# First transfers, first casts and query transposes regrouped in a two-layer decoder trunk

## The chip, the cores and the metric

The kernel runs on one core of a Trainium2 chip. The metric is device time in microseconds (us) of one execution; lower is better. Three runs of the kernel before gave 434.49, 434.71 and 436.08 us, median 434.71 us. Engines are named as the profile names them: PE is the matrix engine (PEld its weight loads), DVE the vector engine, ACT the scalar engine, POOL the GpSimd engine, and SPq the queue of SyncE, which issues most transfers. L12 is line 12 of the kernel before, unless said otherwise.

## What is computed

Two pre-norm mixer layers on x (256 tokens by 1024, float32), then a final RMSNorm. Cut to what matters here:

```python
h = rms_norm(x, norm_g)                       # layer 0
(nq, nkc, nvc, nks, nvs, nkw, nvw, ng, nz, mq, mk, mv, mz, eq, ez) = split(h @ w_in)
a_out = nsa_attention(rot(nq), kc, vc, rot(nks), nvs, rot(nkw), nvw, gates)   # 8 heads, 3 branches
b_out = moba_attention(rot(mq), rot(mk), mv)                                 # 8 heads
m_out = memory_attention(eq, mem_n, w_mem_kv)
x = x + concat(a_out * silu(nz), b_out * silu(mz), m_out * silu(ez)) @ w_out
# layer 1: retention (4 heads) and memory attention, the same outer form; then rms_norm
```

All inputs and the output are float32, and all projections go through PE with each float32 operand split in two.

## The kernel before, in words

**Arithmetic.** A float32 operand is split into a high part (`hi`, a cast to fp32r) and a low part (`lo`, the remainder, again fp32r). A product of two split operands is three matmuls, hi by hi, hi by lo and lo by hi (`mm3`, L243 to L247). For weights, `split` (L141) and, later, `fetch` and `finish` (L157, L170) have ACT write `whi` and then DVE write `wlo`. For x, `gain_cast` (L341) has ACT write `xh`, which is x transposed times the norm's gain, and `gain_low` (L345) has DVE write `xl`. Both are kept in tiles called `big`. The 1024 rows of the contraction are 8 k-tiles of 128.

**The head.** vec (gains, biases), x (transposed) and the weights of the first projection (`ksw`, keys and values of two branches, one half megabyte per two k-tiles) come in by the transfers of L380 to L394: vec and the first two k-tiles of x from ACT's queue, all else from SPq. Six matmuls on a zeroed tile (L397) run on PE meanwhile. Then the loop at L404 to L414 does, for each pair q of k-tiles: two `gain_cast`, two `gain_low`, then for each of the two k-tiles `split` and two `mm3` (token tiles 0 and 1, into the PSUM banks s0 and s1). After each pair but the first, ACT squares the pair before (`square`, L399); POOL adds the squares up (L493, L494), from which the reciprocal root mean square comes by way of PE and DVE, and then computes the angles of layer 1's rotary tables (L485 to L465, helper `angles`). The first pair's casts and the small angle work of layer 0 (L475 to L465 on DVE) share DVE with this loop.

**Buffers.** `raw` (6 buffers) holds transferred pieces, `whi` and `wlo` 4 buffers each. A transfer into a buffer waits on SPq until the buffer's last reader is done. Transfers also take eight completion semaphores in turn: the ninth transfer waits for the landing of the first, and so on.

**Slots.** From L978 on, PE's program is a row of projections. A projection is a generator that yields once per slot (half of a weight unit, 12 matmuls); at each yield `turn` (L188) advances the side tasks, which add their ACT, DVE and PE work at that place. Every engine's order is the order in which the program is written (`manual_schedule`), and each engine works its own list in order. `heads` (L546) is the side task that rotates and transposes queries and keys: per token tile three DVE instructions (`rotate`, L327), then `pause(HP)`, HP = 2 slots, then four PE transposes (L324), then, a slot later, an ACT copy (L556). `sparse_queries` (L722) starts one for the first attention's queries, whose transposes fall into the projection `sparse_gates` that follows; `block_queries` and `block_keys` start two more. `block_values` (L932) leaves its product in two `pj` banks (there are three), and its side task has ACT move both to SBUF (L939); the next projection, `block_gates`, needs one of these banks for its second half.

Of the kernel before, what the change touches and what calls it, by code (L numbers as in the profile page):

```python
# [13 lines left out]
AF = mybir.ActivationFunctionType  # L14
ALU = mybir.AluOpType
AX = mybir.AxisListType

P = 128
T = 256
D = 1024  # L20
KT = 8
# [3 lines left out]
MANUAL = {mybir.EngineType.DVE, mybir.EngineType.Activation, mybir.EngineType.PE, mybir.EngineType.Pool, mybir.EngineType.SP}  # L25
AHEAD = 2
DEPTH = 4
HP = 2
NRAW = 6
NS = 8  # L30
CUT = 256
# [22 lines left out]
V_G0 = 0  # L54
# [8 lines left out]
def trunk(  # L63
# [19 lines left out]
    nc = tc.nc  # L83
    sb = ctx.enter_context(tc.tile_pool(name="sb", bufs=1))
    pp = ctx.enter_context(tc.tile_pool(name="pp", bufs=4, space=bass.MemoryType.PSUM))
    V, S, G, PE = nc.vector, nc.scalar, nc.gpsimd, nc.tensor
# [17 lines left out]
    def load(t, src):  # L104
        nc.sync.dma_start(t, src)
        return t
# [34 lines left out]
    def split(raw, cols):  # L141

        hi = tl("whi", [P, 1024], NB, F32R)[:, :cols]
        lo = tl("wlo", [P, 1024], NB, F32R)[:, :cols]
        S.copy(hi, raw)
        V.tensor_tensor(lo, raw, hi.bitcast(F32), ALU.subtract)
        return hi, lo
# [38 lines left out]
    waiting, first, active, made, slot, free = deque(), [], [], set(), [0], {}  # L186
# [41 lines left out]
    def pause(n):  # L228

        for _ in range(n):  # L230
            yield
# [6 lines left out]
    def making(task, *names):  # L238

        yield from task  # L240
        made.update(names)

    def mm3(ps, lh, ll, rh, rl, start, stop, shared=False):  # L243

        PE.matmul(ps, lh, rh, start=start, stop=False, skip_group_check=shared)  # L245
        PE.matmul(ps, lh, rl, start=False, stop=False, skip_group_check=shared)  # L246
        return PE.matmul(ps, ll, rh, start=False, stop=stop, skip_group_check=shared)  # L247
# [93 lines left out]
    def gain_cast(raw, g, hi, k0, kts):  # L341
        for kt in kts:
            S.activation(hi[:, kt], raw[:, kt - k0], AF.Copy, scale=g[:, kt : kt + 1])  # L343

    def gain_low(raw, g, hi, lo, k0, kts):  # L345
        for kt in kts:
            V.scalar_tensor_tensor(lo[:, kt], raw[:, kt - k0], g[:, kt : kt + 1], hi[:, kt].bitcast(F32),  # L347
                                   op0=ALU.mult, op1=ALU.subtract)
# [4 lines left out]
    vect = tl("vec", [P, V_END])  # L353
# [8 lines left out]
    xh = tl("big", [P, KT, T], 4, F32R)  # L362
# [16 lines left out]
    posr = tl("yf", [P, T], 2, I32)  # L379
    with tc.manual_schedule(engines={mybir.EngineType.SP, mybir.EngineType.Activation}):  # L380
        nc.scalar.dma_start(vect, vec)
        load(wraw[0][:, 0:512], w512[2][:, 0:512])
        for k in range(2):
            nc.scalar.dma_start(xraw[0][:, k : k + 1], xT[:, k : k + 1])
        load(wraw[0][:, 512:1024], w512[2][:, 512:1024])
        S.activation(seed, seed, AF.Sin)
        for q in range(1, 4):
            load(xraw[q // 2][:, 2 * (q % 2) : 2 * (q % 2) + 2], xT[:, 2 * q : 2 * q + 2])
            load(wraw[q], w512[2 + q // 2][:, (q % 2) * 1024 : (q % 2 + 1) * 1024])
        load(cpak, cst)  # L390
        load(posi, pos)
        load(posr, posrow.to_broadcast([P, T]))
        for u in range(4):
            raws.append(load(tl("raw", [P, 1024], NRAW)[:, :560], w280[u // 2][:, u % 2 * 560 : u % 2 * 560 + 560]))  # L394
# [6 lines left out]
        S.activation(squares[q // 2][:, q % 2], xraw[q // 2][:, 2 * (q % 2) : 2 * (q % 2) + 2].rearrange("p k t -> p (k t)"), AF.Square)  # L401

    with tc.manual_schedule(engines=MANUAL):
        for q in range(4):  # L404
            gain_cast(xraw[q // 2], vect[:, V_G0 : V_G0 + 8], xh, 4 * (q // 2), range(2 * q, 2 * q + 2))
            gain_low(xraw[q // 2], vect[:, V_G0 : V_G0 + 8], xh, xl, 4 * (q // 2), range(2 * q, 2 * q + 2))
            for j in range(2):
                wh, wl = split(wraw[q][:, j * 512 : (j + 1) * 512], 512)
                kt = 2 * q + j
                for tok in range(2):  # L410
                    ts = slice(tok * P, (tok + 1) * P)
                    mm3(ps_k[tok], xh[:, kt, ts], xl[:, kt, ts], wh, wl, kt == 0, kt == KT - 1)
            if q:
                square(q - 1)  # L414

    rstd0 = tl("rstd0", [P, 2])
# [126 lines left out]
    szn = tl("v4", [P, 4, T], NV)  # L543


    def heads(ps, name, dst):  # L546

        for tok in range(2):
            while "tab" + name not in made:
                yield  # L550
            r = rotate(ps[tok], tabs[name][0][:, tok], tabs[name][1][:, tok], 8, 32)
            yield from pause(HP)
            tag, = yield from take()
            b = transposes([r[:, i * P : (i + 1) * P] for i in range(4)], tag)
            yield
            S.copy(dst[:, :, tok * P : (tok + 1) * P], b.rearrange("p (k t) -> p k t", t=P))  # L556
            give(tag)
# [164 lines left out]
    def sparse_queries():  # L722
        nonlocal qT
        ps = yield from project((xh, xl))
        qT = tl("v4", [P, 4, T], NV)
        active.append(making(heads(ps, "q", qT), "qT"))

    def compress():
        nonlocal gates, kcBD, vcR
# [202 lines left out]
    def block_values():  # L932
        nonlocal mvt
        ps = yield from project((xh, xl))
        mvt = tl("v4", [P, 2, 512], NV)

        def post():
            for tok in range(2):
                S.activation(mvt[:, tok], ps[tok], AF.Copy, scale=rstd0[:, tok : tok + 1])  # L939
            yield  # L940

        active.append(making(post(), "mvt"))
# [379 lines left out]
```

## Time and profile before

| | |
|---|---|
| median of three runs | 434.71 us (434.49, 434.71, 436.08) |
| profiled execution, its own time | 436.0 us |
| span of its instructions | 434.2 us, granted PE clock 0.992 |
| PE busy | 420.6 us, 97% of the span |
| first matmul of the first projection | starts at 9.38 us |
| first matmul of the second projection that waits (L246, pj) | starts at 23.53 us |
| query transposes of the first attention | start at 46.59 and 54.37 us |

The profile is of one execution. The timeline lists start and duration of instructions, per engine, and in brackets how long the engine stood idle before it and which work ended the idle time. The list of waits adds these up. The chain of waits goes back from the last instruction to whatever released each one.

### The profile page before, as it was taken

What the parts mean: (1) busy time and instruction counts of PE and PEld (TensorE: products, weight loads), DVE (VectorE), ACT (ScalarE), POOL (GpSimd) and SP (SyncE); (2) the same over time, 40 slices, a digit from 0 to 9 for tenths busy, and PEclk for the clock granted to TensorE, in tenths of its full rate; (3) what the DMA queues carried; (4) which work ended last, traced back from release to release, by engine and by line L of the source; (5) the groups of instructions that cost most, each with busy time, mean ns of one, the idle gap of its engine ahead of it and who ended that gap; (6) DMA issues with size and microseconds to landing.
All of it is one profiled execution on the core that took longest, in us unless ns stands there. A gap on an engine that the chain in (4) does not pass through costs nothing.

```text
span 434.2 us, 7030 instructions
## 1 busy us (share of the span) xinstructions
PE 420.6 (97%) x2622; PEld 363.0 (84%) x2622; DVE 307.7 (71%) x666; ACT 243.1 (56%) x453; POOL 18.0 (4%) x24
## 2 busy tenths in 40 slices
PE   6989999999999999999999999999999999999994
PEld 4878888788798987879999988888998888888883
DVE  2897979789597683759777675586887467685634
ACT  4748357676877574737437434646344444545703
POOL 0492000000000000000000000000000000000000
PEclk9899999999999999999999999999999999999998
DMA  8595643444667444526553536555454555655202
GB/s 269 175 329 183 251 163 107 141 141 148 196 206 274 151 109 162 161 85 198 162 195 114 172 131 188 193 201 164 146 171 167 182 190 189 203 171 178 80 0 97
DMA packets 22081, 73.18 MB, mean 169 GB/s; under 512 B 2720, under 2 KB 4000, under 8 KB 22048
## 3 DMA queue, kind: packets, MB, share of 16 engines
q1 hardware_dynamic: 21328, 72.04, 50.2%
q10 hardware_dynamic: 720, 0.71, 0.6%
q8 instruction: 20, 0.33, 0.3%
q14 instruction: 13, 0.11, 0.1%
HBM read 71.69 MB, written 1.05 MB: 168 GB/s over the span
## 4 chain that ended last, share of the span: by engine, by line
PE 84%; DVE 6%; POOL 3%; ACT 2%; DMA 2%; issue 1%; ACTq 0%; DVEq 0%; POOLq 0%
PE pj L245 22%; PE pj L247 21%; PE pj L246 21%; PE o L117 3%; PE s L117 2%; DVE wlo L174 2%; PE t L324 2%; PE s L324 2%; DMA raw<-in_xT 2%; PE s L246 1%; PE s L247 1%; PE tr L245 1%; PE tr L246 1%; PE tr L247 1%; PE s L245 1%
## 5 line engine op out<-in xcount | busy, mean ns | idle before, releaser
L174 DVE TENSOR_TENSOR wlo<-raw,whi 128x1024 fp32r<-128x1024 f32 (+1 forms) x118 | 142.5, 1211 | 63.0 <-ACT whi L166 60.9
L166 ACT CAST whi<-raw 128x1024 fp32r<-128x1024 f32 (+1 forms) x118 | 121.7, 1036 | 89.6 <-PE pj L247 38.3
L245 PE MATMUL pj<-whi,big 128*128 128x512 f32 (+2 forms) x256 | 97.4, 383 | 0.0
L246 PE MATMUL pj<-wlo,big 128*128 128x512 f32 (+2 forms) x256 | 96.1, 375 | 0.8 <-DVE wlo L174 0.8
L247 PE MATMUL pj<-whi,big 128*128 128x512 f32 (+2 forms) x256 | 95.9, 375 | 0.0
L245 PE MATMUL pj<-big,whi 128*128 128x256 f32 x256 | 73.6, 288 | 0.6 <-ACT v L939 0.6
L247 PE MATMUL pj<-big,wlo 128*128 128x256 f32 x256 | 72.6, 284 | 0.0
L246 PE MATMUL pj<-big,whi 128*128 128x256 f32 x256 | 72.5, 283 | 0.0
L245 PEld LDWEIGHTS pj<-whi,big 128*128 128x128 f32 x256 | 48.2, 188 | 9.3 <-issue 1.5
L246 PEld LDWEIGHTS pj<-wlo,big 128*128 128x128 f32 x256 | 48.3, 189 | 8.8 <-DVE wlo L174 1.1
L247 PEld LDWEIGHTS pj<-whi,big 128*128 128x128 f32 x256 | 48.2, 188 | 8.7
L245 PEld LDWEIGHTS pj<-big,whi 128*128 128x128 f32 x256 | 49.0, 191 | 2.7 <-issue 1.8
L246 PEld LDWEIGHTS pj<-big,whi 128*128 128x128 f32 x256 | 49.0, 191 | 0.1
L247 PEld LDWEIGHTS pj<-big,wlo 128*128 128x128 f32 x256 | 49.0, 191 | 0.0
L610 ACT ACTIVATE p<-p,mx 128x128 f32<-128x128 f32 (+1 forms) x48 | 21.2, 443 | 4.5 <-DVE mx L597 4.4
L245 PE MATMUL pj<-whi,y 128*128 128x512 f32 x42 | 16.9, 407 | 0.0
L247 PE MATMUL pj<-whi,y 128*128 128x512 f32 x42 | 16.4, 391 | 0.0
L246 PE MATMUL pj<-wlo,y 128*128 128x512 f32 x42 | 16.2, 391 | 0.0
L347 DVE SCALAR_TENSOR_TENSOR big<-raw,vec,big 128x256 fp32r<-128x256 f32 x16 | 7.8, 526 | 8.0 <-ACT big L343 8.0
L572 DVE TENSOR_SCALAR p<-p,sm 128x256 f32<-128x256 f32 (+1 forms) x48 | 12.7, 322 | 0.6
L570 ACT ACTIVATE p<-p,sm 128x256 f32<-128x256 f32 (+1 forms) x16 | 7.8, 489 | 7.9 <-DVE sm L566 7.5
L597 DVE CUSTOM_DVE_ANT_0 p<-s,cst 128x128 f32<-128x128 f32 (+1 forms) x24 | 7.1, 354 | 5.8 <-PE s L117 5.8
(350 smaller groups left out, 668.4 us busy)
## 6 DMA issues: line engine op xcount, KB each, us to landing
raw<-in_w SPq DMA_DIRECT2D x91, 512.0 KB, 3.9
raw<-in_wout SPq DMA_DIRECT2D x28, 512.0 KB, 4.2
raw<-in_w SPq DMA_DIRECT2D x4, 280.0 KB, 2.9
v<-in_w SPq DMA_DIRECT2D x2, 512.0 KB, 5.9
raw<-in_memT SPq DMA_DIRECT2D x2, 512.0 KB, 3.8
raw<-in_memtok SPq DMA_DIRECT2D x2, 512.0 KB, 4.8
v<-in_xtok SPq DMA_DIRECT2D x2, 512.0 KB, 5.5
v<-in_grow SPq DMA_DIRECT2D x2, 512.0 KB, 6.8
```

What stands on the lines that cost most here:

```text
L117: ins = PE.matmul(out, lhs, rhs, start=start, stop=stop)
L166: S.copy(hi, raw)
L174: V.tensor_tensor(lo, raw, hi.bitcast(F32), ALU.subtract)
L245: PE.matmul(ps, lh, rh, start=start, stop=False, skip_group_check=shared)
L246: PE.matmul(ps, lh, rl, start=False, stop=False, skip_group_check=shared)
L247: return PE.matmul(ps, ll, rh, start=False, stop=stop, skip_group_check=shared)
L324: PE.transpose(b[:, i * P : (i + 1) * P], a, ident)
L347: V.scalar_tensor_tensor(lo[:, kt], raw[:, kt - k0], g[:, kt : kt + 1], hi[:, kt].bitcast(F32), op0=ALU.mult, op1=ALU.subtract)
L570: S.activation(p[:, hh, a], p[:, hh, a], AF.Copy, scale=sm[:, hh, tok : tok + 1])
L572: V.tensor_scalar(p[:, hh, a], p[:, hh, a], sm[:, hh, tok : tok + 1], None, op0=ALU.mult)
L597: V.tensor_tensor_reduce(ps[i][:, hh, a], ss[i][hh][:, a], cpak[:, C_CAUSAL + a.start : C_CAUSAL + a.stop], -1.0, 3e38, ALU.add, ALU.min, ...
L610: S.activation(ps[i][:, hh, a], src, AF.Exp, bias=ms[i][:, hh, tok : tok + 1], scale=-1.0 if causal else 1.0, accum_out=ns[i][:, hh, tok : ...
```

## The change

Four edits, and one that only renames:

1. The first two k-tiles of x come in one transfer of 256 KB from ACT's queue instead of two of 128 KB; it is issued in the place of the first. SPq's list of transfers is as before, but since there is one transfer less, the semaphores that they wait for shift by one.
2. The loop of the head goes k-tile by k-tile: `split`, one `gain_cast`, one `gain_low`, and then the six matmuls with the token tile as the inner loop (hi by hi for both token tiles, then lo of the weights, then lo of x).
3. The queries of the first attention pause three slots instead of two before each pair of transposes; all others stay at two (the constant HP becomes a default argument).
4. In `block_values` DVE moves the first token tile's product, ACT the second.

```diff
-HP = 2
...
         nc.scalar.dma_start(vect, vec)
+        nc.scalar.dma_start(xraw[0][:, 0:2], xT[:, 0:2])
         load(wraw[0][:, 0:512], w512[2][:, 0:512])
-        for k in range(2):
-            nc.scalar.dma_start(xraw[0][:, k : k + 1], xT[:, k : k + 1])
         load(wraw[0][:, 512:1024], w512[2][:, 512:1024])
...
-        for q in range(4):
-            gain_cast(xraw[q // 2], vect[:, V_G0 : V_G0 + 8], xh, 4 * (q // 2), range(2 * q, 2 * q + 2))
-            gain_low(xraw[q // 2], vect[:, V_G0 : V_G0 + 8], xh, xl, 4 * (q // 2), range(2 * q, 2 * q + 2))
-            for j in range(2):
-                wh, wl = split(wraw[q][:, j * 512 : (j + 1) * 512], 512)
-                kt = 2 * q + j
+        for kt in range(KT):
+            q, j = kt // 2, kt % 2
+            wh, wl = split(wraw[q][:, j * 512 : (j + 1) * 512], 512)
+            gain_cast(xraw[q // 2], vect[:, V_G0 : V_G0 + 8], xh, 4 * (q // 2), (kt,))
+            gain_low(xraw[q // 2], vect[:, V_G0 : V_G0 + 8], xh, xl, 4 * (q // 2), (kt,))
+            for i, (x, w) in enumerate(((xh, wh), (xh, wl), (xl, wh))):
                 for tok in range(2):
-                    ts = slice(tok * P, (tok + 1) * P)
-                    mm3(ps_k[tok], xh[:, kt, ts], xl[:, kt, ts], wh, wl, kt == 0, kt == KT - 1)
-            if q:
+                    PE.matmul(ps_k[tok], x[:, kt, tok * P : (tok + 1) * P], w, start=kt == 0 and i == 0,
+                              stop=kt == KT - 1 and i == 2)
+            if q and j:
                 square(q - 1)
...
-    def heads(ps, name, dst):
+    def heads(ps, name, dst, wait=2):
...
-            yield from pause(HP)
+            yield from pause(wait)
...
-        active.append(making(heads(ps, "q", qT), "qT"))
+        active.append(making(heads(ps, "q", qT, 3), "qT"))
...
         def post():
-            for tok in range(2):
-                S.activation(mvt[:, tok], ps[tok], AF.Copy, scale=rstd0[:, tok : tok + 1])
+            V.tensor_scalar(mvt[:, 0], ps[0], rstd0[:, 0:1], None, op0=ALU.mult)
+            S.activation(mvt[:, 1], ps[1], AF.Copy, scale=rstd0[:, 1:2])
             yield
```

**ACT at the start of the program**, before. raw_76 is x's first half, raw_77 the weights of the first two k-tiles, raw_78 those of the next two, big_72 is `xh`:

```order
L381 DMA vec_63<-in_vec 128x104
L384 DMA raw_76<-in_xT 128x256 x2
L386 ACT_TABLE_LOAD
L386 ACTIVATE seed_61<-seed_61 128x1
L343 ACTIVATE big_72<-raw_76,vec_63 128x256 x2
L145 CAST whi_82<-raw_77 128x512
L145 CAST whi_144<-raw_77 128x512
```

And with the change (whose lines from L380 to L399 stand one or two lower):

```order
L380 DMA vec_63<-in_vec 128x104
L381 DMA raw_76<-in_xT 128x512
L384 ACT_TABLE_LOAD
L384 ACTIVATE seed_61<-seed_61 128x1
L144 CAST whi_82<-raw_77 128x512
L342 ACTIVATE big_72<-raw_76,vec_63 128x256
L144 CAST whi_141<-raw_77 128x512
L342 ACTIVATE big_72<-raw_76,vec_63 128x256
```

The first weight cast now stands ahead of x's first cast, and the second of each behind the first pair.

**DVE at the end of the head**, before. big_73 is `xl`, wlo_209 and wlo_219 belong to the last two k-tiles, wlo_243 to the first unit of the second projection; tmp and posf are layer 0's angles:

```order
L475 CAST posf_234<-pos_64 128x2
L347 SCALAR_TENSOR_TENSOR big_73<-raw_79,vec_63,big_72 128x256
L477 TENSOR_SCALAR tmp_27_90<-cst_65,posf_234 128x32 x2
L146 TENSOR_TENSOR wlo_209<-raw_81,whi_208 128x512
L456 TENSOR_SCALAR tmp_54_231<-tmp_27_90 128x64
L146 TENSOR_TENSOR wlo_219<-raw_81,whi_218 128x512
L457 TENSOR_SCALAR tmp_54_231<-tmp_54_231 128x64
L461 SCALAR_TENSOR_TENSOR tmp_27_90<-tmp_54_231,tmp_27_90 128x64
L174 TENSOR_TENSOR wlo_243<-raw_114,whi_242 128x560
```

With the change:

```order
L473 CAST posf_233<-pos_64 128x2
L145 TENSOR_TENSOR wlo_204<-raw_81,whi_203 128x512
L475 TENSOR_SCALAR tmp_27_90<-cst_65,posf_233 128x32 x2
L346 SCALAR_TENSOR_TENSOR big_73<-raw_79,vec_63,big_72 128x256
L145 TENSOR_TENSOR wlo_216<-raw_81,whi_215 128x512
L454 TENSOR_SCALAR tmp_54_230<-tmp_27_90 128x64
L346 SCALAR_TENSOR_TENSOR big_73<-raw_79,vec_63,big_72 128x256
L455 TENSOR_SCALAR tmp_54_230<-tmp_54_230 128x64
L173 TENSOR_TENSOR wlo_242<-raw_113,whi_241 128x560
```

The last `xl` stands behind the last `wlo` of the head, and one of the three L461 moves behind the second projection's first `wlo`. On PE, in turn, the second projection's first matmul moves ahead of the head's last two, which need that `xl`.

**PE at the first query transposes** (t_570 before, t_582 with the change), inside `sparse_gates`; s_114 and s_115 are its two banks, whi_486 and whi_485 the same weight unit under two names. Before:

```order
L246 MATMUL s_115_510<-big_73,whi_445 128x256
L247 MATMUL s_115_510<-big_72,wlo_446 128x256
L324 MATMUL t_570<-cst_65,rot_a_518 128x128 x4
L245 MATMUL s_114_509<-big_72,whi_486 128x256
L246 MATMUL s_114_509<-big_73,whi_486 128x256
```

With the change:

```order
L245 MATMUL s_114_508<-big_73,whi_485 128x256
L246 MATMUL s_114_508<-big_72,wlo_486 128x256
L323 MATMUL t_582<-cst_65,rot_a_517 128x128 x4
L244 MATMUL s_115_509<-big_72,whi_485 128x256
L245 MATMUL s_115_509<-big_73,whi_485 128x256
```

The first four transposes move from ahead of this unit's first half to behind it (12 matmuls), the second four by 24 matmuls, since the second pause follows the first; each of the two ACT copies moves behind one more weight cast. All else in PE's program behind the head stands as before.

## The prediction, made before the change was run

> **What bounds the kernel now.** I read the page's first lines, then the list of PE's waits, because it says what of the span is not matmul.
>
> ```profile
> span 434.2 us, 7030 instructions
> PE 420.6 (97%) x2622; PEld 363.0 (84%) x2622; DVE 307.7 (71%) x666; ACT 243.1 (56%) x453; POOL 18.0 (4%) x24
> ...
> PE s L245 <- ACT whi L145: 2.6, 1, 2.6
> PE t L324 <- DVE rot_a L338: 1.1, 2, 0.8
> PE pj L245 <- ACT v L939: 0.6, 1, 0.6
> ```
>
> PE works 97% of the span, and the change neither adds nor removes a matmul. So only PE's waits (total, times, longest) can be won, and the time at which PE stops waiting for good. The three quoted lie at places that the change edits. The chain of waits and the windows (stretch, length, PE busy, granted clock, DMA share, GB/s) show the first of them:
>
> ```profile
> 1.66 6.63 DMA raw<-in_xT
> ...
> 7.45:10.85 3.40, 1.25 (x4) 1.00 1.03 401
> 10.85:14.25 3.40, 3.40 (x9) 0.50 0.97 320
> ...
> 1.31 5.49 PE L397 MATMUL t<-p 128*128 128x256 f32 x12 [1.31 <-POOL p L357]
> 9.38 0.50 PE L245 MATMUL s<-whi,big 128*128 128x512 f32 x1 [2.58 <-ACT whi L145]
> 23.53 0.40 PE L246 MATMUL pj<-wlo,big 128*128 128x280 f32 x1 [0.76 <-DVE wlo L174]
> ```
>
> The second piece of x lands at 8.3 us, the casts follow, and PE starts at 9.38 after 2.58 us of idling behind the six warm-up matmuls (over at 6.80). In the 3.40 us from 10.85 on the granted clock is 0.50. But PE's late start is not what sets the end: at 23.53 PE waits again, for DVE. Whatever the head saves has to get past that point.
>
> **The change, part by part.** The sum goes against the profiled execution: 436.0 us, 434.2 of span and 1.8 around it.
>
> *x in one transfer.* Issue times and times from issue to landing (last number):
>
> ```profile
> 1.18 0.93 ACTq L384 DMA_DIRECT2D raw<-in_xT  x2
> 2.11 0.43 SPq L105 DMA_DIRECT2D raw<-in_w  x1
> ...
> raw<-in_xT ACTq DMA_DIRECT2D x1, 128.0 KB, 4.9
> ...
> raw<-in_xT SPq DMA_DIRECT2D x1, 256.0 KB, 5.4
> ...
> raw<-in_w SPq DMA_DIRECT2D x1, 512.0 KB, 6.6
> ```
>
> The new transfer is issued at 1.18. Its bounds are the landing of the old first piece, 6.1 (1.18 + 4.9), and that of the half megabyte queued behind it, 8.7 (2.11 + 6.6). I take the row of the same size and row length, 5.4 us: landing at 6.6. Then `xh` of the first k-tile is done at 7.1 and PE starts there, 2.2 us earlier, 0.3 us after the warm-up. The weights of k-tiles 2 and 3 still land at 8.7, since the bytes ahead of them are the same; ACT will have two k-tiles done by about 8.1 and wait for them. That landing, not x, sets the pace from there, so x may come up to 7.3 without cost. One transfer less also lets the third weight piece go out without waiting for vec's landing; the queue is full then anyway, so I count nothing.
>
> *k-tile by k-tile.* ACT's and DVE's work is the same, in another order. Start to start in these rows, a cast takes 0.515 us, a gain 0.405, a square 0.53, and PE's six matmuls of a k-tile 1.36 (17.72 to 19.08):
>
> ```profile
> 9.75 0.91 ACT L343 ACTIVATE big<-raw,vec 128x256 fp32r<-128x256 f32 x2
> 10.56 1.12 ACT L145 CAST whi<-raw 128x512 fp32r<-128x512 f32 x2
> 11.59 0.63 ACT L401 ACTIVATE v<-raw 128x512 f32<-128x512 f32 x1
> 12.12 0.89 ACT L343 ACTIVATE big<-raw,vec 128x256 fp32r<-128x256 f32 x2
> 17.76 0.62 ACT L401 ACTIVATE v<-raw 128x512 f32<-128x512 f32 x1
> 17.72 0.39 PE L245 MATMUL s<-whi,big 128*128 128x512 f32 x1
> 19.08 0.39 PE L245 MATMUL s<-whi,big 128*128 128x512 f32 x1
> ...
> ACT whi L145 <- PE s L247: 1.2, 2, 1.0
> ```
>
> From 8.75 on that is 0.92 a k-tile: k-tiles 2 and 3 and the first square to 11.1, 4 and 5 with the second square to 13.5, 6 and 7 with the third to 15.9. The third square ended at 18.38 (17.76 + 0.62), so ACT is 2.4 us earlier. The 1.2 us for which ACT waited for PE's `whi` buffers go, because PE, from 7.1 on and at full clock, has released each buffer long before. PE alone would end the head near 18.1 (7.1 + 8 × 1.36).
>
> DVE does not follow. POOL's additions and DVE exclude one another:
>
> ```profile
> 18.54 3.18 POOL L493 TENSOR_TENSOR v<-v,v 128x512 f32<-128x512 f32 x2 [1.49 <-ACT v L401]
> 21.80 0.74 POOL L494 TENSOR_TENSOR v<-v 128x256 f32<-128x256 f32 x1
> 22.48 0.40 POOL L485 CAST tmp<-yf 128x256 f32<-128x256 int32 x1
> 22.98 1.33 POOL L486 TENSOR_SCALAR tmp<-tmp,cst 128x256 f32<-128x256 f32 x1
> 10.57 0.87 DVE L347 SCALAR_TENSOR_TENSOR big<-raw,vec,big 128x256 fp32r<-128x256 f32 x2
> 19.85 0.68 DVE L146 TENSOR_TENSOR wlo<-raw,whi 128x512 fp32r<-128x512 f32 x1
> 20.45 1.31 DVE L457 TENSOR_SCALAR tmp<-tmp 128x64 f32<-128x64 f32 x1
> 22.54 0.93 DVE L174 TENSOR_TENSOR wlo<-raw,whi 128x560 fp32r<-128x560 f32 x1
> ```
>
> The 64-column L457, begun at 20.45, ends at 21.76, when POOL's two L493 are over (18.54 + 3.18 = 21.72); and the second of them, begun beside a `wlo`, took 1.8 us of the 3.18. I lay the two engines out in turn, an L493 at 1.25 (half of 3.18 less the 0.6 of that `wlo`, about), a `wlo` at 0.6 (19.85 to 20.45), an `xl` at 0.4 (half of 0.87): the second L493 starts at 16.3 (third square at 15.9, DVE's turn to 16.3), ends at 17.55; last `wlo` to 18.15; third L493 to 19.4; the small L454 and the last `xl` to 19.85; L494 (0.74) to 20.6; the second projection's first `wlo` (0.74, the 0.68 of 512 columns times 560/512) to 21.4. Before it ended at 23.47 (22.54 + 0.93). PE resumes **2.1 us** earlier, with the same matmuls done. Ends: 0.9, if two more POOL instructions, L485 and L486, get in ahead of that `wlo` (0.40, and 1.33 less the 0.49 for which the `wlo` held it up to 23.47: 1.2 together); and 2.4, ACT's lead, if POOL holds up nothing. More does not last: ACT stands in line for POOL's angles later on, and POOL starts on them with its own lead, 22.54 less 20.6, 1.9 us.
>
> *Queries a slot later.*
>
> ```profile
> 46.59 0.65 PE L324 MATMUL t<-cst,rot_a 128*128 128x128 f32 x4 [0.28 <-DVE rot_a L338]
> 48.51 0.28 PE L245 MATMUL s<-big,whi 128*128 128x256 f32 x1
> 49.95 0.28 PE L245 MATMUL s<-big,whi 128*128 128x256 f32 x1
> 54.37 0.63 PE L324 MATMUL t<-cst,rot_a 128*128 128x128 f32 x4 [0.83 <-DVE rot_a L338]
> ```
>
> A slot of twelve matmuls lasts 1.44 us (48.51 to 49.95), over the 0.28 and, with two slots, the 0.83 us waited: **1.1 us** go. Late next would be the ACT copy that makes the second queries; but a half unit, 1.44 us, and the start of the next projection still stand between these transposes and the first scores, and an ACT instruction of 512 columns takes 0.63 (the square at 11.59). Ends: 1.1 and 0.3, the latter if PE's lead outgrows DVE's by 0.8.
>
> *Products moved by DVE and ACT.*
>
> ```profile
> 109.58 0.75 DVE L572 TENSOR_SCALAR p<-p,sm 128x128 f32<-128x128 f32 x3
> 111.12 1.23 DVE L174 TENSOR_TENSOR wlo<-raw,whi 128x1024 fp32r<-128x1024 f32 x1 [0.79 <-ACT whi L166]
> 112.21 1.29 ACT L939 ACTIVATE v<-pj,rstd 128x512 f32<-128x512 f32 x2
> 112.97 0.39 PE L245 MATMUL pj<-big,whi 128*128 128x256 f32 x1 [0.60 <-ACT v L939]
> ```
>
> PE needs the first token tile's bank, freed in the first half of L939's 1.29 us. DVE does that move in the hole from 110.33 to 111.12. A 512-column DVE instruction takes 0.69 us (the `wlo` above, 0.68), so it ends at 111.0, long before PE's 112.37, and the `wlo` behind it starts on time. ACT's copies behind L939 come 0.6 us earlier too, so the attention products behind them follow. **0.6 us**; ends 0.6 and 0.3.
>
> Sum: 436.0 − 2.1 − 1.1 − 0.6 = **432.2 us**. The median run is 1.3 under the profiled one, and two of three runs lie at 434.5 to 434.7 while one, at 436.08, is like the profile. I read the 1.4 us between them as the half-clock stretch: without it ACT waits 1.2 us less for PE. In such runs the head wins 0.7 instead of 2.1 and the end is the same. The Trainium skill, TensorE: Matmul & The Clock Gate, Part 1, has the clock set by windows of about 3.4 us that run freely and so fall differently from run to run; the stretch of 3.40 us here agrees, and that some runs escape it no trace here can show. 432.2 is 0.58% under the median of 434.71; 0.5%, 2.2 us, is about what a measurement can tell from no change.
>
> **The rivals.**
>
> *The offset is not the clock.* If profiled executions simply take 1.3 us longer, all 3.8 us come off the median: 430.9. For it: the profile is one execution. Against: one unprofiled run has the same time.
>
> *The clock falls in the new gaps.* By the layout above PE, ahead of DVE, works only 1.9 of the 5 us from 16.4 to 21.4 (four pairs of matmuls at 0.227 and the next projection's first). The windows above show 1.25 busy of 3.40 us, then 0.50. A stretch of 3.4 us at half clock costs 1.7: 433.9. Against: each single gap is 1.2 us or less, the one before was 2.58. The same page of the Trainium skill, in "Why this matters for your kernels", asks only for no gap over about 3 us between bursts; by that rule the clock would hold and 432.2 stand, but the 2.58 us gap of this trace already lost it.
>
> *x lands with the weights behind it*, at 8.7, as its old second piece nearly did: everything on ACT is 1.4 us later, 433.6. For it: that piece, issued at 1.66, took 6.63.
>
> *Slower.* In the head, on DVE: POOL's L485 and L486 slip ahead of the second projection's first `wlo` (2.1 becomes 0.9), PE's idle time before it grows by 1.2 us, and by that the clock falls (1.7): 432.2 + 1.2 + 1.7 = 435.1. It decides from about 1.2 us of PE work in 3.4.
>
> *The change doesn't do what it says* only in one sense, that DVE eats the head's gain as against a full-clock run: it is the 433.6 case.
>
> **How the numbers follow.** Forecast 0.50 (its own spread 431.4 to 432.9, some six tenths of it below 432.5), offset 0.18, clock 0.14, late x 0.11, slower 0.07. Faster by over 0.5% means below 432.5: 0.31 + 0.18 and a little, 0.50. Slower by over 0.5% means above 436.9: 0.03, of the last case's tail. The rest, 0.47, is within. The range 430.8 to 434.3 leaves out the last case and the ends of two others, under 0.2.
>
> **What would show it.** x's transfer landing near 6.6 and the first matmul at 7.1; no stretch at 0.50 in the head; the third square ending near 15.9; the first `wlo` of the second projection ending near 21.4, with PE idling for DVE ahead of it; no wait at the queries' transposes and none behind L939. I am wrong if the first `wlo` ends above 22.5, if the clock shows 0.50 after 17 us, or if a new wait of over half a microsecond stands between 55 and 112 us.

## The result, and the profile after

The changed kernel takes **431.37 us** (median of four runs, 431.23 to 431.43) against 435.15 for the old one on the same chip (434.49 to 436.08): ratio 0.991, 95% interval 0.989 to 0.993, so 0.9% faster. The profiled execution goes from 436.0 to 431.38, its span from 434.2 to 429.6: 4.6 us, where the sum of the prediction had 3.8. Two runs of the experiments below, 464.99 us in e2 and 521.63 in e3, had mean granted clocks of 0.85 and 0.75 and are left out of every median and range.

PE's waits in the changed kernel (total, times, longest), with lines one or two lower than before:

```profile
PE s L409 <- ACT big L342: 1.6, 1, 1.6
PE t L395 <- POOL p L356: 1.3, 1, 1.3
PE tr L504 <- DVE rstd L137: 1.1, 1, 1.1
PE pj L245 <- DVE wlo L173: 1.1, 1, 1.1
PE tr L323 <- DVE p L570: 0.3, 1, 0.3
PE s L409 <- DVE big L346: 0.3, 1, 0.3
```

The waits at the queries' transposes (1.1) and behind `block_values` (0.6) are gone. The one ahead of the head is 1.6 instead of 2.6. Two have grown: the second projection's first `wlo` (0.8 to 1.1) and L504 (0.5 to 1.1), PE's *spreading matmul*, which needs the reciprocal root `rstd` that DVE computes. The windows (stretch, length, then busy time of PE, PEld, DVE, ACT and POOL, granted clock, DMA share, GB/s) and the timeline of the changed kernel:

```profile
7.45:10.85 3.40, 3.40 (x16) 2.79 (x16) 2.98 (x7) 2.96 (x7) 0.00 (x0) 1.00 1.05 421
10.85:14.25 3.40, 3.40 (x17) 2.81 (x16) 3.13 (x7) 3.40 (x9) 0.80 (x1) 1.00 0.97 351
17.60:21.00 3.40, 1.97 (x11) 1.21 (x10) 3.37 (x7) 0.98 (x2) 3.24 (x4) 1.00 0.84 284
...
1.31 4.27 PE L395 MATMUL t<-p 128*128 128x256 f32 x12 [1.31 <-POOL p L356]
7.22 0.72 PE L409 MATMUL s<-whi,big 128*128 128x512 f32 x2 [1.64 <-ACT big L342]
15.11 0.62 ACT L399 ACTIVATE v<-raw 128x512 f32<-128x512 f32 x1
15.88 3.60 POOL L491 TENSOR_TENSOR v<-v,v 128x512 f32<-128x512 f32 x2 [1.09 <-ACT v L399]
18.26 1.27 DVE L455 TENSOR_SCALAR tmp<-tmp 128x64 f32<-128x64 f32 x1
19.45 0.73 DVE L173 TENSOR_TENSOR wlo<-raw,whi 128x560 fp32r<-128x560 f32 x1
19.55 1.35 POOL L492 TENSOR_TENSOR v<-v 128x256 f32<-128x256 f32 x1
20.23 0.40 PE L245 MATMUL pj<-wlo,big 128*128 128x280 f32 x1 [1.11 <-DVE wlo L173]
29.65 0.71 PE L504 MATMUL tr<-cst,rstd 128*128 128x128 f32 x4 [1.11 <-DVE rstd L137]
31.42 0.40 POOL L463 TENSOR_SCALAR tmp<-tmp 128x256 f32<-128x256 f32 x1
```

No stretch at half clock, and the head begins at 7.22. The first `wlo` ends at 20.18, not 23.47, and PE resumes 3.30 us earlier. But the spreading matmul, for which PE waits in both kernels, stands at 29.65 against this row of the old one:

```profile
32.20 0.71 PE L506 MATMUL tr<-cst,rstd 128*128 128x128 f32 x4 [0.47 <-DVE rstd L138]
33.97 0.40 POOL L465 TENSOR_SCALAR tmp<-tmp 128x256 f32<-128x256 f32 x1
```

So 2.55 us get past it, and POOL's last angle instruction (L465, now L463) also ends 2.55 earlier, at 31.82 instead of 34.37. The first attention scores begin 3.84 earlier (61.64 to 57.80), which adds 1.3 at the queries; `block_values` adds 0.6. That is 4.4 of the 4.6.

### The profile page after: what moved, and what is told of

Read it like the earlier page. It is cut to its first block, busy times and chain, and to the rows that moved or that the text cites. A ratio compares the mean times of both kernels' runs of the same rounds, so it can differ in the third digit from the quotient of the medians.

```text
span 429.6 us, 7028 instructions
## 1 busy us (share of the span) xinstructions
PE 417.7 (97%) x2622; PEld 361.1 (84%) x2622; DVE 308.1 (72%) x667; ACT 242.3 (56%) x452; POOL 18.1 (4%) x24
## 4 chain that ended last, share of the span: by engine, by line
PE 88%; DVE 7%; DMA 1%; issue 1%; ACT 1%; SPq 0%; DVEq 0%
PE pj L244 23%; PE pj L246 22%; PE pj L245 22%; PE o L116 4%; DVE wlo L173 2%; PE s L116 2%; PE s L323 2%; PE t L323 2%; DMA raw<-in_w 1%; PE s L244 1%; PE s L246 1%; PE s L245 1%; PE tr L244 1%; PE tr L246 1%; PE tr L245 1%
## 5 line engine op out<-in xcount | busy, mean ns | idle before, releaser
L409 PE MATMUL s<-whi,big 128*128 128x512 f32 x32 | 9.0, 396 | 2.0 <-ACT big L342 1.6
```

The costliest lines, as they stand in the source:

```text
L409: PE.matmul(ps_k[tok], x[:, kt, tok * P : (tok + 1) * P], w, start=kt == 0 and i == 0, stop=kt == KT - 1 and i == 2)
```

## The experiments

Each kernel was timed beside the old one on the same chip. The column "POOL's end" is the end of POOL's last angle instruction, "spreading" the start of PE's spreading matmul, both in the one profiled execution, in us from the span's start.

| kernel | median (range), us | old kernel's median | POOL's end | spreading | span |
|---|---|---|---|---|---|
| old | 435.15 (434.49–436.08) | | 34.37 | 32.20 | 434.2 |
| changed | 431.37 (431.23–431.43) | 435.15 | 31.82 | 29.65 | 429.6 |
| e1, edit 2 alone | 434.77 (434.52–435.53) | 435.20 | 33.26 | 29.27 | 433.1 |
| e2, edit 1 alone | 434.52 (433.22–435.69) | 435.20 | 32.90 | 30.73 | 432.6 |
| e3, longer warm-up | 435.82 (435.51–436.11) | 435.20 | 34.02 | 30.03 | 433.9 |
| e4, edits 3 and 4 | 432.63 (431.45–433.27) | 435.20 | 33.42 | 31.24 | 431.5 |
| f1, edits 1 and 2 | 433.43 (433.23–433.61) | 434.97 | 31.68 | 29.51 | 431.4 |
| f2, edit 2, sines later | 432.97 (432.38–434.02) | 434.97 | 33.90 | 29.92 | 431.8 |
| f3, edits 3, 4, warm-up | 433.86 (433.51–434.79) | 434.97 | 31.29 | 32.88 | 433.0 |
| f4, small DVE work later | 434.51 (434.02–435.59) | 434.97 | 30.95 | 31.02 | 432.4 |
| g1, spreading later | 431.46 (431.12–431.82) | 435.14 | 31.75 | 29.63 | 429.7 |
| g2, one instruction ahead | 432.35 (431.42–433.06) | 435.14 | 32.13 | 29.96 | 430.2 |
| g3, no L492 on POOL | 430.96 (430.80–432.82) | 435.14 | 31.11 | 28.94 | 429.0 |
| h1, both later | 430.69 (430.56–431.25) | 434.97 | 31.85 | 29.74 | 428.9 |

### The edits one by one, and the clock by itself

**e1** is the old kernel with the loop of edit 2:

```diff
-        for q in range(4):
-            gain_cast(..., range(2 * q, 2 * q + 2))
...
+        for kt in range(KT):
+            wh, wl = split(...)
+            gain_cast(..., (kt,))
+            gain_low(..., (kt,))
+            ... six matmuls, token tile inside
```

> The old kernel with only the second edit, the head's loop k-tile by k-tile; x still comes in two pieces. Theory (the order of the loop carries the head's gain, because the weights of k-tiles 2 and 3, which land at 8.5, set ACT's pace and not x): the first k-tile needs only the first piece of x, PE starts near 7.1, the second piece lands at 8.3 and delays ACT by no more than 0.3 us, the clock stays at 1.00 through the head, the first wlo of the second projection ends near 20.4 (20.2 with all edits, 23.5 without), and the median is 1.7 us (edits 3 and 4) above that of the full change and a little: 433.1 to 433.5. Rival (x in one transfer is what brings the start forward): the casts wait for the second piece, the wlo ends at 22 or later, and the median is 434 or above.

**e2** has edit 1 alone:

```diff
+        nc.scalar.dma_start(xraw[0][:, 0:2], xT[:, 0:2])
         load(wraw[0][:, 0:512], w512[2][:, 0:512])
-        for k in range(2):
-            nc.scalar.dma_start(xraw[0][:, k : k + 1], xT[:, k : k + 1])
```

> The old kernel with only the first edit, x's first two k-tiles in one transfer; the head's loop as before. Theory: x lands at 6.6, both gains and then both weight casts follow, the first matmul stands at 8.2 instead of 9.38, but ACT then has the order of before and the first wlo of the second projection ends 1.0 to 2.0 us earlier than 23.5 (1.1 from the start, up to 1.2 more if the clock does not fall, since the gap behind the warm-up shrinks from 2.6 to about 1.4): median 433.4 to 434.2. Rival (x is what counts): the wlo ends near 20.5 as with the whole change and the median is 433.1. Rival (the transfer makes no difference without the loop): within 0.3 us of before.

**e3** keeps PE busy up to the head:

```diff
-    for _ in range(6):
+    for _ in range(9):
         PE.matmul(wb[:, :256], warm[:, 0:P], warm[:, :256], start=True, stop=True)
```

> The old kernel with nine warm-up matmuls instead of six, so that PE idles less than 0.7 us, not 2.58, before the head's first matmul; nothing else. Theory (the 1.5 us between runs of the old kernel are the half-clock stretch in the head, which falls in some runs only): no stretch at 0.50 after 9 us, all runs near the old kernel's fastest, 434.3 to 434.7, none at 435.5 or above. Rival (the spread has another cause, and a profiled run is simply longer): the runs spread from 434.5 to 436 as before, whatever the clock shows.

**e4** has `heads(ps, "q", qT, 3)` and the split `post()` of `block_values`, as in the change, in the old kernel.

> The old kernel with only the third and fourth edits (queries turned a slot later, DVE moves the first token tile's product); the head as before. Theory: 1.1 and 0.6 us, with no wait left at either place, so 1.7 us below the old kernel of the same runs, whose two levels (434.5 and 436) both stay and become 432.8 and 434.3. Rival (the waits come back elsewhere, as a wait for the ACT copy of the second queries or behind DVE's next wlo): 0.5 to 1.0 us.

None of the four medians came out as the theory had it; e1's lies where its rival put it, at 434 or above, though its first `wlo` ends at 21.56 and not at 22 or later. Neither half of the head's change does much alone: 0.43 us for the loop (ratio 0.9989, interval 0.9976 to 1.0001), 0.7 for the transfer (0.9987, 0.9975 to 1.0000). The runs of e2 fall into two groups, three at 433.2 to 433.4 and eight at 434.4 to 435.7; no trace shows one of the three, so what sets them apart stays open. e3, at full clock throughout its head, is no faster: its runs lie in the upper half of the old kernel's (ratio 1.0018, 1.0010 to 1.0027). But e3 is not a clean test of the clock. Layer 0's angles and the `wlo` of the second projection are written in two different scheduling blocks (L979 and L971 to L974), and the build interleaves them on DVE by a plan of its own. With three more matmuls it put the last L461 and L465 ahead of the second projection's first `wlo`, where the old kernel had them behind it:

```profile
18.28 1.45 DVE L461 SCALAR_TENSOR_TENSOR tmp<-tmp,tmp 128x64 f32<-128x64 f32 x2
19.76 1.30 DVE L465 TENSOR_SCALAR tmp<-tmp 128x64 f32<-128x64 f32 x1
20.99 3.42 DVE L174 TENSOR_TENSOR wlo<-raw,whi 128x560 fp32r<-128x560 f32 x4
```

e4, whose DVE order there is the old one, gives 2.6 us, more than its two waits. In its profiled execution, the slowest of its six runs, POOL's end is 0.95 earlier than in the old kernel's; span less POOL's end is 398.1, against 399.8, a difference of the 1.7 expected. That is an argument and not a measurement: f3 below, with the same two edits, does not keep this difference (401.7). By the medians the two edits alone are worth 2.6 (2.0 to 3.1 by the interval, 0.9928 to 0.9955), and why more than 1.7 is not shown.

The trace of e1 says where its head's gain went: POOL, ACT behind it, and PE at the queries' transposes:

```profile
16.21 4.62 POOL L493 TENSOR_TENSOR v<-v,v 128x512 f32<-128x512 f32 x2 [1.10 <-ACT v L401]
32.80 0.46 POOL L465 TENSOR_SCALAR tmp<-tmp 128x256 f32<-128x256 f32 x1
33.29 0.42 ACT L467 ACTIVATE trig<-tmp 128x256 f32<-128x256 f32 x1 [2.73 <-POOL tmp L465]
29.27 0.71 PE L506 MATMUL tr<-cst,rstd 128*128 128x128 f32 x4 [1.02 <-DVE rstd L138]
45.47 0.66 PE L324 MATMUL t<-cst,rot_a 128*128 128x128 f32 x4 [1.56 <-DVE rot_a L338]
```

PE's spreading matmul is 2.9 us earlier than in the old kernel, but POOL's end only 1.1: its pair of additions took 4.62 us instead of 3.18, beside a DVE whose small instructions stood a place earlier than in the changed kernel. ACT stands 2.73 us at L467, the sine of POOL's angles, with a gain of the keys, a weight cast and the queries' tables behind it. In the old kernel and in e1, e2 and e3 alike PE's first transposes start 12.2 us after POOL's end (33.26 and 45.47 here), so PE's lead is waited off: 1.56 us instead of 0.28, and 0.83 again. In the table, span less POOL's end is 399.8 for the old kernel, 399.8 for e1, 399.7 for e2 and 399.9 for e3. That became the theory of the next group: **without edit 3 the kernel follows POOL's end, not PE's head.**

### Does POOL's end set the time?

**f1** is edits 1 and 2 together, so that only 3 and 4 are missing.

> The old kernel with the first and second edits together (x in one transfer, the loop k-tile by k-tile), the third and fourth left out. Theory now (POOL's angles: the end of POOL's last L465 sets when ACT goes on, and 12.15 us after it the first rotated queries are ready, in every trace so far; what the head gives PE is lost at the queries' transposes unless POOL is earlier too): POOL ends near 31.8 as with the whole change, the first rot_a is ready at 44.0, PE arrives at 43.6 and waits 0.4 and 0.8, so the head's gain gets through and the median is 1.2 + 0.6 above the whole change, 433.0 to 433.4. Rival (the head alone is lost as in each half alone, because only PE is earlier): waits of 2 us or more at these transposes and 434.3 to 434.8.

**f2** is e1 with the two sines of POOL's angles two slots later in ACT's line:

```diff
-AT = {..., "rsin": 10, ...}
+AT = {..., "rsin": 12, ...}
```

> The old kernel with the second edit and, besides, ACT's two sines of POOL's angles two slots later (they are for the second layer), so that ACT does not stand in line for POOL with a gain of the keys, a weight cast and the queries' tables behind it. With the second edit alone PE waited 1.56 and 0.83 us for the rotated queries and 0.33 for the keys. Theory (ACT behind POOL's angles holds the queries): these waits fall to 1.0 us together or less without the third edit, and the median to 432.1 to 433.3 from 434.77. Rival (DVE's own queue holds the queries, or PE's queries come no earlier): the waits stay at 2 us or more and the median within 0.4 of 434.77.

**f3** is e4 with the nine warm-up matmuls of e3.

> The old kernel with the third and fourth edits and nine warm-up matmuls instead of six, which keeps the clock at 1.00 in the head. The third and fourth edits alone gave runs from 431.45 to 433.27. Theory (what counts is when POOL is done, and a full clock without another loop order did not bring POOL forward: 34.0 instead of 34.4): 432.6 to 433.5 in all runs, with a spread under 0.7. Rival (the half clock is what costs, now that no wait at the transposes hides it): 431.3 to 431.8 in all runs, as the whole change.

**f4** is the changed kernel with DVE's small instructions for layer 0's angles ordered behind the fourth `wlo` of the second projection:

```diff
-        V.tensor_copy(posf, posi)
+        tc.add_manual_dep(V.tensor_copy(posf, posi).ins, lows[3].ins.name, ... NoSync ...)
```

> The changed kernel with DVE's seven small instructions for the angles of layer 0 moved behind the four halves (wlo) of the second projection; nothing else. Theory (64-column instructions of 0.2 us take 1.3 beside POOL's additions, and two of them stand ahead of the first wlo): that wlo ends near 17.5 instead of 20.2, PE's waits of 1.1 and 0.3 us there go, and part of it comes back as a longer wait of the spreading matmul (1.1 now) or, if POOL's end stays at 31.8, at the queries: median 430.0 to 430.9 from 431.37. Rival (the small instructions fill time in which DVE waits for ACT): within 0.3 of the changed kernel.

f1 came out as expected, 0.03 above the range: POOL's end at 31.68, waits of 0.28 and 0.83, 433.43 us, and span less POOL's end 399.7 once more. So the two halves of the head's change, worth 0.4 and 0.7 alone, are worth 1.5 together (ratio 0.9967, 0.9956 to 0.9979). That this is more than their sum of 1.1 is not shown: 1.1 lies inside the interval, which is 0.9 to 1.9 us. What the traces show is that only the two together, in the DVE order that the build gives them, leave POOL's pair of additions early and no longer than 3.62 (from 15.71 on; e1 16.21 and 4.62, e2 16.98 and 3.29).

f2 is the direct test. POOL ends at 33.90, later than in e1, and yet the kernel is 2.0 us under the old one, where e1 was 0.4 under it. Its list of PE's waits begins:

```profile
PE s L411 <- ACT big L343: 1.4, 2, 1.0
PE t L397 <- POOL p L357: 1.3, 1, 1.3
PE tr L506 <- DVE rstd L138: 1.0, 1, 1.0
PE t L324 <- DVE rot_a L338: 0.8, 1, 0.8
```

The wait of 1.56 at the first transposes is gone and so is that for the keys; only the second, 0.83, stays. Span less POOL's end is 397.9. ACT's line behind POOL was what held the queries, as the theory had it.

f3 lies 0.4 above what the theory gave and far above the rival's 431.3 to 431.8, and the theory's premise did not hold: POOL's end came forward, to 31.29, where 34.0 was expected. It has e3's order on DVE and so does not test the clock cleanly either. In its profiled execution, the slowest of its twelve runs, the clock was kept at the head's start and lost at its end, behind PE's wait of 1.98 us for a `wlo` at 20.18. The windows of f3:

```profile
17.60:21.00 3.40, 1.42 (x7) 0.87 (x6) 3.40 (x5) 0.91 (x2) 3.24 (x4) 1.00 0.17 64
21.00:24.40 3.40, 3.40 (x10) 2.65 (x9) 3.33 (x7) 0.66 (x1) 3.13 (x4) 0.51 0.46 145
```

With POOL early (31.29) and edit 3 in place, its time follows PE: span less the spreading matmul is 400.1, against 399.9 in the changed kernel and 400.3 in e4.

f4 was expected to gain, and is back at the old kernel's level (ratio 0.9996, 0.9984 to 1.0007). PE resumed 0.76 earlier, with that first `wlo` itself held up by POOL, but the small work, 2.8 us of it, now stood between the four halves and the chain to `rstd`:

```profile
31.02 0.71 PE L506 MATMUL tr<-cst,rstd 128*128 128x128 f32 x4 [3.36 <-DVE rstd L137]
...
27.80:31.20 3.40, 0.18 (x1) 0.18 (x2) 3.29 (x7) 0.14 (x1) 3.14 (x6) 1.00 0.59 206
31.20:34.60 3.40, 3.40 (x13) 2.73 (x13) 3.33 (x8) 3.37 (x12) 0.37 (x2) 0.65 0.78 247
```

PE waits 3.36 us there, and the granted clock falls behind it. Here an earlier first `wlo` gained nothing; DVE's work up to `rstd` is what PE's lead runs into.

### What holds the changed kernel

**g1** moves the spreading matmul half a weight unit later:

```diff
         yield from until(AT["spread"])
-        for tok in range(2):
-            PE.matmul(b[:, tok * P : (tok + 1) * P], rstd0[...], ident, start=True, stop=True)
...
         made.add("tabk")
         yield
+        for tok in range(2):
+            PE.matmul(b[:, tok * P : (tok + 1) * P], rstd0[...], ident, start=True, stop=True)
+        yield
         S.copy(rb0, b[:, :T])
```

> The changed kernel with PE's spreading matmul (which waits for DVE's reciprocal root, 1.11 us) half a weight unit later, ahead of ACT's copy of its result; the tables' scalings stay. Theory (in the head of the changed kernel DVE's chain to rstd sets PE's time, and nothing else stands close behind it: the keys' rotation is ready 1.1 us before PE needs it, the queries' 1.05): the wait goes, up to 1.1 us come off, perhaps 0.1 to 0.3 of it back at the keys or queries: median 430.2 to 430.7 from 431.37. Rival (PE only arrives earlier at the next thing that DVE or ACT has late): within 0.3 of 431.37, with a new wait between 29 and 46 us.

**g2** puts one of the three L459 ahead of the first `wlo` by an ordering edge on DVE, like f4's.

> The changed kernel with one small DVE instruction (the first of the three L459 of layer 0's angles) ahead of the second projection's first wlo, where the old kernel had it, so that POOL's last addition can get in ahead of that wlo as my layout had it. Theory (that end of the first wlo does not set the end of the kernel; DVE's chain to rstd does, whose work is the same): the wlo ends 0.7 to 1.2 us later, PE's wait ahead of it grows by as much and its wait at the spreading matmul shrinks by as much; that matmul stays at 29.4 to 30.0 and the median within 0.4 of 431.37. Rival (the first wlo sets PE's time, as my prediction had it): 432.0 to 432.6.

**g3** takes the addition of the two halves from POOL:

```diff
-        G.tensor_tensor(sq[:, :T], sq[:, :T], sq[:, T:], ALU.add)
...
-            PE.matmul(b[:, 256 + tok : 257 + tok], sq[:, tok * P : (tok + 1) * P], ones, start=True, stop=True)
+            for k in range(2):
+                PE.matmul(b[:, 256 + tok : 257 + tok], sq[:, k * T + tok * P : ...], ones, start=k == 0, stop=k == 1)
```

> The changed kernel without POOL's addition of the two halves of the squares (L492, 0.74 us and up to 1.35 beside DVE); PE does it with two more matmuls of one column. Theory (POOL and DVE hold each other up, so DVE's chain and POOL's angles both come earlier): POOL's last L463 ends 0.7 to 1.3 us earlier than 31.8, DVE's rstd 0.2 to 0.7 earlier than 29.6, the spreading matmul as much earlier, and the median 430.7 to 431.3. Rival (POOL's place is only taken by its next instruction, L483 and L484, which hold DVE up in turn): rstd within 0.2 us, the median 431.3 to 431.6.

In g1 the wait of 1.1 is gone and the time is the same: 431.46. The rival held, but for the place: a wait that the changed kernel does not have stands at 48.4, behind the 46 that it named, at the matmuls of the compressed keys, which need DVE's eight products L775 (L774 in the changed kernel, whose two rows come second):

```profile
44.95 3.34 DVE L775 TENSOR_TENSOR tmp<-o,vec 64x240 f32<-64x240 f32 x8
48.39 2.06 PE L116 MATMUL o<-tmp,v 128*64 128x30 f32 x64 [0.91 <-issue]
...
45.03 3.34 DVE L774 TENSOR_TENSOR tmp<-o,vec 64x240 f32<-64x240 f32 x8
48.47 2.06 PE L116 MATMUL o<-tmp,v 128*64 128x30 f32 x64
```

The profile names no releaser of that wait (`issue`); that it is the products is read from the times, since in both kernels the matmuls start 0.10 us after the products' end. In the changed kernel these end at 48.37 (45.03 + 3.34) and PE reaches them at 48.47, with nothing to spare. So, as the next theory had it, two things bind it at once: the chain to `rstd`, and POOL's end by way of ACT and DVE.

g2 shows who decides at 19.5 us. With one small instruction between L455 and the `wlo`, POOL's addition gets in:

```profile
19.67 0.72 POOL L496 TENSOR_TENSOR v<-v 128x256 f32<-128x256 f32 x1
19.68 0.80 DVE L460 SCALAR_TENSOR_TENSOR tmp<-tmp,tmp 128x64 f32<-128x64 f32 x1
20.40 0.93 DVE L174 TENSOR_TENSOR wlo<-raw,whi 128x560 fp32r<-128x560 f32 x1
21.39 0.39 PE L246 MATMUL pj<-wlo,big 128*128 128x280 f32 x1 [2.14 <-DVE wlo L174]
```

The `wlo` ends 1.15 us later (21.33), but the spreading matmul only 0.31 (29.96) and the profiled span 0.6: most of the slip is taken up by the shorter wait at the spread, as the theory had it. The median, 432.35, is 1.0 above the changed kernel's, in the rival's range. Its runs spread from 431.42 to 433.06, and the three above 432.6 have the lowest mean granted clocks (0.992 and 0.993, against 0.996 in the two fastest); so a part may be the clock. In the profiled run, 432.03, it held through the wait of 2.14 us, and no trace shows one of the slower three, so g2 does not decide between the two:

```profile
17.60:21.00 3.40, 1.18 (x5) 0.41 (x3) 3.37 (x5) 1.09 (x2) 3.14 (x5) 1.00 0.80 290
```

g3 brings POOL's end forward by 0.71 and the spreading matmul by as much, and the median to 430.96, in the range expected. The profiled span is 0.6 shorter; the ratio's interval (0.9892 to 0.9924) overlaps that of the changed kernel.

**h1** has g1's move and f2's later sines in the changed kernel.

> The changed kernel with both: the spreading matmul half a unit later, and ACT's two sines of POOL's angles two slots later, so that neither DVE's chain to rstd nor POOL's angles hold the way to the queries. Theory (two things bind at once in the changed kernel: the spreading matmul on PE, and POOL's end by way of ACT and DVE, whose last link are DVE's products for the compressed keys, for which PE waited 0.91 us when only the first was taken away): with both gone the 1.1 us come through, 430.1 to 430.7, with no wait at the compression's matmuls. Rival (the way to the products is DVE's own work, not ACT's line behind POOL): the wait of 0.9 stays there and the median within 0.3 of 431.37.

Its median is the lowest of all, 430.69 (ratio to the old kernel 0.9899, 0.9877 to 0.9920; the changed kernel 0.9911, 0.9890 to 0.9932). The spans, 428.9 against 429.6, say 0.7 less; the intervals overlap, so that it is faster than the changed kernel is likely and not shown. The wait at the compression fell, but not to nothing:

```profile
44.48 3.34 DVE L775 TENSOR_TENSOR tmp<-o,vec 64x240 f32<-64x240 f32 x8
47.92 2.06 PE L116 MATMUL o<-tmp,v 128*64 128x30 f32 x64 [0.50 <-issue]
```

The products come 0.55 earlier than in the changed kernel, and not 1.1; half the expected gain was had. What holds them next is ACT's casts and its table load ahead of the `wlo` at 39.75, by the timeline; whether that is so stays open.

## Why the prediction was right, and where not

**What bounds the kernel**: right. PE's busy time is the same, and all of the gain is waits and clock.

**x in one transfer; the start.** Landing 6.6, first matmul 7.1: measured 6.6 and 7.22. No stretch at 0.50, the third square ending at 15.73 (15.9 was forecast), and the weights of k-tiles 2 and 3, at 8.51, for which ACT waits 0.45: all as laid out. But PE did not start 0.3 us behind the warm-up: that was over at 5.58 (1.31 + 4.27) instead of 6.80, and PE idled 1.64 us. In e2 the clock fell behind a gap of that size, 1.60 us, so the clock's holding here does not rest on the short gap that was forecast:

```profile
7.81 0.50 PE L245 MATMUL s<-whi,big 128*128 128x512 f32 x1 [1.60 <-ACT whi L145]
...
7.45:10.85 3.40, 2.82 (x7) 2.08 (x8) 3.38 (x7) 3.40 (x8) 0.00 (x0) 0.71 1.02 403
```

**The first `wlo` at 21.4**: 20.18. The step that failed is the place of L494 (now L492) ahead of that `wlo`. L455 was over together with POOL's pair at 19.5, the `wlo` stood right behind it and took the turn 0.1 us before L492; and the last `xl` and L454 had been done inside the pair, not after it. That is 0.74 and some 0.45 of the 1.2. g2 puts one instruction between, and POOL gets the turn.

**The head's term of 2.1**: mis-sized, 2.55. It was also read at the wrong place. PE's resumption moved by 3.30 and 0.6 of it was waited off at the spreading matmul, where PE waited before too. There and at POOL's end the kernel takes its time from; both moved by 2.55. The prediction named the right limit ("ACT stands in line for POOL's angles") but gave POOL a lead of 1.9. The lead at the end of L492 is less than that, 1.64 (22.54 to 20.90); the other 0.91 came off the angles themselves, which ran beside other work of DVE (the first L463 of the old kernel takes 1.91 us, its like 1.26; L456 0.69 and 0.42).

**The queries, 1.1, and `block_values`, 0.6**: by the trace right in size, no wait left at either place and 1.8 us of span between f1 and the changed kernel; by the medians more (e4 2.6), for which no run gives the reason. They were added as if independent of the head, which holds only because POOL's end moved with PE. Where the head moves PE alone (e1, e3), the queries' waits grow from 1.1 to 2.4 us; an edit there is then worth that much more, and the head's edit as much less.

**432.2 for the median run.** Against the profiled execution 4.6 us came off instead of 3.8, to 431.38; from median to median it was 3.78 (435.15 to 431.37). The reading that the old kernel's runs differ by the clock in the head, and that the head wins only 0.7 in those that keep it, holds as a correlation: of 74 runs of the old kernel on four occasions, the 8 with a mean granted clock of 0.998 or more took 433.7 to 434.1, the 16 with 0.989 or less 435.6 to 436.8. From 433.9 the changed kernel's 431.37 is 2.5 away, which leaves 0.8 for the head if edits 3 and 4 are worth 1.7. But the profiled execution itself does not fit: with a mean clock of 0.992 it took 436.0, where the 16 of the 74 runs with 0.992 took 434.7 to 435.3. And the mean also counts the end of the program, where PE has no work: the changed kernel's clock is 1.00 from 7.45 to 34.60 in its windows and yet 0.998 in the mean, with 0.50 in the last 1.6 us. As a cause the clock is not shown: e1 and e3, whose windows show 1.00 throughout the head, have no run below 434.52 and 435.51, with POOL's ends at 33.26 and 34.02, but another order on DVE too. What POOL does in the old kernel's fastest runs was not traced, so whether the clock or the turns of DVE and POOL make them fast stays open. The changed kernel's runs lie within 0.2 us, e4's, with the old head, within 1.8. The fastest of e4, 431.45, is as fast as the changed kernel: of the 1.26 us between the medians, much is that every run is as fast as that one.

**The rivals.** *Offset*: its 430.9 is nearer than 432.2, but its mechanism is wrong. The changed kernel's profiled execution, 431.38, lies among its other runs (431.23 to 431.43), so a profiled run is not longer as such. That the old kernel's was slow among its runs stays true. *The clock in the new gaps*: PE worked 1.97 of the 3.40 us from 17.6 and the clock held; with 1.42 in f3 it fell, and with 1.18 in g2 it held. The Trainium skill (TensorE: Matmul & The Clock Gate, "Why this matters for your kernels") asks for no gap over about 3 us between bursts; the 1.98 of f3, like the 2.58 of the old kernel and the 1.60 of e2, lost the clock, so the measurement decides against that figure. Since the 2.14 of g2 kept it, neither the length of the gap nor the busy time of such a window decides alone. The forecast's measure, about 1.2 us of PE work in 3.4, fails as well (1.42 fell, 1.18 held): that the clock holds here was forecast rightly, but what decides it stays open. *Late x* and *slower by L485 and L486*: neither came; DVE got ahead of L492 instead.

## What to carry to other kernels

Where an engine waits twice in a row, size an edit ahead of both at the second wait, since a gain at the first is waited off there. Ask which engine that is not waited for directly stands at the start of the line (here POOL, for sines that are needed a layer later), and test it with a difference that stays constant over kernels, such as span less that engine's end; then cut the link, as f2 does, since a constant difference alone shows no cause. Edits whose gains one by one can hardly be told from nothing (intervals up to 1.0001 and 1.0000) can give a clear one together (0.9967), so trying each alone would have dropped the head of this change.

## What the runs showed that was not expected

DVE and POOL take turns, and who gets the turn depends on a tenth of a microsecond. From the start of POOL's pair of additions to the end of its angles took 15.8 to 16.0 us in the old and the changed kernel, e2, e4 and f1, but 17.1 to 17.2 in e1, e3 and f2, and 14.6 in f3, whose DVE had the same work in a slightly other order. The 64-column L455 of one input took 1.27 us beside POOL and ended with POOL's pair (19.53 and 19.48). Its like in e1, begun 0.13 us after that kernel's pair, took 0.18; there the pair took 4.62 us:

```profile
16.34 0.18 DVE L456 TENSOR_SCALAR tmp<-tmp 128x64 f32<-128x64 f32 x1
```

The Trainium skill (SBUF — State Buffer, "Who interferes with whom") has the shared port as a lock that is held for the whole instruction, with `tensor_scalar` among those that can take it; the rows of L455 and L491 agree.

An edit far from DVE's queue changed its order: three more warm-up matmuls on PE, or x in one transfer instead of two, moved DVE's small instructions by a place or two in the build's plan; e3 came out 0.6 us slower than the old kernel. An experiment on such a kernel has to compare the orders as well as the traces.
